# A streaming encoder layer on one core: the convolution's mean emitted later, sample heads turned later, taps held at a block's first head

## The chip, the cores and the metric

The kernel runs on one core of a Trainium2 chip. The metric is the device time of one execution in microseconds (us). A core has TensorE (matrix products, PE in the profile; PEld is its weight load), VectorE (DVE), ScalarE (ACT), GpSimd (POOL) and SyncE (SP, which only issues DMAs here). Each engine works through its own list of instructions in order, and waits on semaphores for the others.

## The reference

One layer of a hybrid encoder, on 2048 prompt frames and 64 sample frames, D_MODEL 1024. All is float32; the kernel gets that accuracy from products of split operands (a high and a low part).

```python
h = rms_norm(x, norm1_g) * (1 + sc1) + sh1          # modulated by c
glu_a, glu_b, q, k, v, g_conv, g_attn = split(h @ w_in)
u = glu_a * sigmoid(glu_b)
y = depthwise_conv(concat(hist, u), w_dw) + b_dw    # 31 taps, 512 channels
conv_out = silu(layer_norm(y)) @ w_conv_out         # mean and variance over channels
q, k = rms_norm per head(q), rms_norm per head(k)   # 8 heads of 64
o = band attention(q, k, v)                         # own chunk of 64 and the 8 before, bias, softmax
merged = sigmoid(g_conv) * conv_out + sigmoid(g_attn) * (o @ w_attn_out)
x = x + gt1 * (merged @ w_o)
x = x + gt2 * swiglu_ffn(rms_norm(x) modulated)
```

The sample frames attend to 256 cached keys and their own 64. Outputs are both x, the last 30 convolution inputs, and the keys and values kept for the next step.

## The kernel before, in words

The work has two phases. The first (to about 1220 us) goes through four token blocks: block 0 has the 64 sample rows and 512 prompt rows, blocks 1 to 3 have 512 prompt rows each. Each block runs the stages q, 0, k, 1, v, 2, 3, g: the projections to q, k and v (21 us of TensorE each, `ps<-whi,hh` and its like in the profile), four channel tiles of the gated linear unit (stages 0 to 3, `ps<-hh,whi`), and 16 gate columns (g). The second phase is the merge, the output projection and the feed-forward network, which the change does not touch.

These stages are a plain loop over TensorE's products. Everything else is woven in by a planner at build time. `Stream` keeps an estimate of each engine's load (line 163 on) and calls `tick` after each 500 ns of planned products; `tick` pumps five lanes (`Lane`, line 110): `norm_lane` (the next block's row norms), `work` (norms of q and k), `attn` (heads), `tail` (the convolution's layer norm) and `conv` (the taps). A lane holds generators. A generator yields the planned time at which it may go on, or a test; `pump` steps the first one that is ready, while the engines named in the lane's `room` are not too far ahead of TensorE. `drain` steps a lane to its end whatever the due times. The order in which instructions are emitted gives their priority to a scheduler behind it, which fixes each engine's list. Generators emit their instructions through helpers with one line (L105 in the profile), so the profile is read here by tiles.

The parts that the change touches:

- `convolve(u, y, ct, b)` (line 1224): for one channel tile one tensor_scalar and 30 fused multiply-adds on VectorE (`y<-u,wd,y`, 0.75 us for 512 columns, 0.84 for 606), one lane step each; lane `conv`, room 2000 ns on VectorE, up to four steps a tick.
- `conv_norm(y, c0, n, t0)` (line 1244), lane `tail`: waits until the `conv` lane is empty, then in all blocks but the last for MEAN_LAG. Then three additions on POOL (`s<-y`, `s<-s,y`), a product with a matrix of 1/512 that gives every partition the mean (`pm<-s,ones`), four subtractions, four squares on ScalarE, three additions on POOL (`s<-s,ln`), a second such product for the variance, square root, four reciprocals, four multiplications on POOL (`y<-y,s`), and per channel tile tanh, scale, product, split and two stores to c_d. Block 0 has two of these, first the sample's 64 columns, then the prompt's 512. Stage 0 of the next block begins with `conv.drain()` and `tail.drain()`, as `y` has one buffer.
- `attend(i)` (line 1449), lane `attn`, two heads at a time. In block 0 prompt and sample heads alternate: (0, head 0), (s, head 0), (0, head 1) and so on. A head is scored tile by tile (`sc<-kk,q` on TensorE, the maximum `pr<-sc,bias` on VectorE, the exponential on ScalarE; the tile sc has one buffer), then `scored` is set and the next head's operands are fetched. When the last tile is scaled (`pr<-pr,sm`), the head is turned: transposes (`ptp<-ident,pr`), split (`ph`, `pl`), products with V (`po<-ph,vv`), `finish_head` and the stores to o_d. Between scaling and turning it waits until TensorE's planned time has passed ScalarE's by PE_LAG.
- `heads(b)` (line 1587): 2 us after stage v it drains `work` and adds the block's heads to `attn`. At gate column 10 of block 3 (`SIDE_G`) the `conv` lane is drained.

Of the kernel before, what the change touches and what calls it, by code (L numbers as in the profile page):

```python
# [43 lines left out]
PE_LAG = 400.0  # L44
TURN_LAG = 2500.0
KN_LAG = 5000.0
X_LAG = 8000.0
MEAN_LAG = 10000.0
ON_POOL = ()
DMA_LAG = 4000.0  # L50
OUT_LAG = 4000.0
# [36 lines left out]
class Meter:  # L88


    def __init__(self, engine, name, stream):
        self.engine, self.name, self.stream = engine, name, stream
# [17 lines left out]
class Lane:  # L110
# [2 lines left out]

    def __init__(self, room, spacing=0.0, wide=1, burst=1):
        self.gens, self.room, self.spacing, self.wide, self.burst = [], room, spacing, wide, burst
        self.last = -1e9

    def add(self, gen):
        self.gens.append([gen, 0.0, {}])
# [23 lines left out]
    def pump(self, stream):  # L143
        for _ in range(self.burst):
            now = stream.load["pe"]
            if now - self.last < self.spacing or stream.full(self.room):
                return
            entry = next((e for e in self.gens[: self.wide] if self.ready(e, stream)), None)
            if entry is None:
                return  # L150
            self.last = now
            self.step(entry)
# [438 lines left out]
def streaming_layer(ctx: ExitStack, tc: tile.TileContext, I, O):  # L591
    nc = tc.nc
    stream = Stream()
    pe, dve, act, gps = (
        Meter(e, n, stream) for e, n in ((nc.tensor, "pe"), (nc.vector, "dve"), (nc.scalar, "act"), (nc.gpsimd, "pool"))
    )
# [28 lines left out]
    now = {}  # L625
# [618 lines left out]
    def conv_norm(y, c0, n, t0):  # L1244
        yv = y[:, :, c0 : c0 + n]
        yield lambda: not conv.gens
        if t0 < PBLOCKS[-1][0]:
            yield stream.load["pe"] + MEAN_LAG
        s = wk.tile([P, 512], F32, tag="ln_s", bufs=1)
# [150 lines left out]
    def spans(b):  # L1400

        if b == "s":
            return 0, SMP, 0, CACHE + SMP
        past = QB if b else 0
        return SMP + QB * b, QB, CACHE + SMP + QB * b - past, QB + past
# [11 lines left out]
    def attention(b):  # L1417

        plan(b)
        for i, head in enumerate(order):  # L1420
            if head[0] == b or b == 0:
                attn.add(attend(i))

    def plan(b):

        if (b, 0) not in order:
            order.extend((x, h) for h in range(NH) for x in ((0, "s") if b == 0 else (b,)))
# [21 lines left out]
    def attend(i):  # L1449
        x, h = order[i]  # L1450
        q0, nq, k0, nk = spans(x)
        yield lambda: now["scored"] == i - 1
        fetch(i)
        fetch_v(i)
        yield loaded[i]
        (q2, kk), (_, bias), vnow = now["qk", i], now["bias"], now["v", i]
        tiles = []
        for t in range(0, nq, P):
            n = min(P, nq - t)
            if x != 0 or t % (2 * P) == 0:  # L1460
                both = ps_a.tile([P, 2, 512], F32, tag="s", name="sc")
            ps = both if x != 0 or t % (2 * P) == 0 else both[:, 1:]
            if x not in (0, "s"):
                for j in range(2):
                    for d in range(2):
                        pe.matmul(ps[:, j, :320], q2[:, d, t : t + P], kk[:, t + 320 * j : t + 320 * j + 320], start=d == 0, stop=d == 1)
                w, src, bs = 640, ps[:, :, :320], bias[:, ::-1]
            else:
                w = nk if x == "s" else t + P
                for d in range(2):  # L1470
                    pe.matmul(ps[:n, 0, :w], q2[:, d, t : t + n], kk[:, :w], start=d == 0, stop=d == 1)
                src, bs = ps[:n, 0:1, :w], bias[:n, 64:384][:, ::-1] if x == "s" else bias[:, :w][:, ::-1]
            pr, sm, free, ready = softmax_max(src, n, w, bs)
            tiles.append((pr, sm, n, w))
            if x == 0 and t % (2 * P) == 0:
                yield stream.load["pe"], SCORE_ROOM
            elif t + P < nq:
                yield free + PE_LAG, SCORE_ROOM
            else:
                fetch(i + 1)  # L1480
                now["scored"] = i
            if t:
                softmax_scale(*tiles[-2])
        yield ready
        softmax_scale(*tiles[-1])
        yield stream.when("act") + PE_LAG
        while now["finished"] < i - 1:
            yield lambda: now["finished"] == i - 1
        fetch_v(i + 1)
        po = ps_a.tile([P, 512], F32, tag="o", name="po")  # L1490
        if x == "s":
            pt = ps_g.tile([P, 512], F32, tag="gp", name="ptp")
            ph = wk.tile([P, 512], F32R, tag="ph", name="ph", bufs=3)
            pl = wk.tile([P, 512], F32R, tag="pl", name="pl", bufs=3)
            js = ((0, P), (1, P), (2, SMP))
            for j, m in js:
                c = slice(j * SMP, j * SMP + SMP)
                pe.transpose(pt[:m, c], tiles[0][0][:SMP, j * P : j * P + m], ident[:SMP, :SMP])
            stream.after("act", "pe")
            split(ph[:, : 2 * SMP], pl[:, : 2 * SMP], pt[:, : 2 * SMP])  # L1500
            split(ph[:SMP, 2 * SMP : 3 * SMP], pl[:SMP, 2 * SMP : 3 * SMP], pt[:SMP, 2 * SMP : 3 * SMP])
            yield stream.when("dve") + PE_LAG
            for j, m in js:
                c = slice(j * SMP, j * SMP + SMP)
                for y_ in (ph, pl):
                    pe.matmul(po[:, :SMP], vnow[:m, j], y_[:m, c], start=j == 0 and y_ is ph, stop=j == 2 and y_ is pl)
        else:
            seq = (0, 1, 2, 3) if x == 0 else (3, 4, 0, 1, 2)

            def av(jj, ph, pl, _):  # L1510
                if x:
                    uses = [(jj, 0, min(jj, 3) + 1)] + ([(jj + 5, jj + 1, 4)] if jj < 3 else [])
                else:
                    uses = [(jj, jj, 4)]
                for j, a, e in uses:
                    for y_ in (ph, pl):
                        pe.matmul(
                            po[:, a * P : e * P], vnow[:, j], y_[:, a * P : e * P], start=jj == seq[0] and y_ is ph,
                            stop=jj == seq[-1] and y_ is pl and j == uses[-1][0], skip_group_check=True,
                        )  # L1520

            pend = []
            for jj in seq:
                if len(pend) > 2:
                    yield pend[0][3] + PE_LAG
                    av(*pend.pop(0))
                pt = ps_g.tile([P, 512], F32, tag="gp", name="ptp")
                t0 = 0 if x else jj
                for t in range(t0, 4):
                    j = (jj - t + (5 if t > jj else 0)) if x else jj  # L1530
                    pe.transpose(pt[:, t * P : t * P + P], tiles[t][0][:, j * P : j * P + P], ident)
                ph = wk.tile([P, 512], F32R, tag="ph", name="ph", bufs=3)
                pl = wk.tile([P, 512], F32R, tag="pl", name="pl", bufs=3)
                stream.after("act", "pe")
                w = 512 - t0 * P
                if x in ON_POOL and jj % 2:
                    p32 = temp("p32")
                    act.activation(p32[:, :w], pt[:, t0 * P :], AF.Copy)
                    act.activation(ph[:, t0 * P :], p32[:, :w], AF.Copy)
                    stream.after("pool", "act")  # L1540
                    gps.tensor_tensor(pl[:, t0 * P :], p32[:, :w], ph[:, t0 * P :].bitcast(F32), ALU.subtract)
                    pend.append((jj, ph, pl, stream.when("pool")))
                else:
                    split(ph[:, t0 * P :], pl[:, t0 * P :], pt[:, t0 * P :])
                    pend.append((jj, ph, pl, stream.when("dve")))
                yield
            for args in pend:
                yield args[3] + PE_LAG
                av(*args)
        yield stream.when("pe")  # L1550
        yield from finish_head(h, po, SMP if x == "s" else QB, q0, "s" if x == "s" else "p")
        now["finished"] = i
# [4 lines left out]
    conv, tail = Lane({"dve": CONV_ROOM}, burst=4), Lane({})  # L1557
# [17 lines left out]
    for b, stage in ORDER:  # L1575
# [7 lines left out]
        elif stage in ("q", "k", "v"):  # L1583
            qkv(b, "qkv".index(stage), norms)
            if stage == "v":

                def heads(b=b):
                    work.drain()
                    stream.flush()
                    attention(b)  # L1590
                    if b == 3:
                        attn.burst, attn.spacing = 2, 0.0

                stream.at(stream.load["pe"] + HEADS_NS, heads)
# [617 lines left out]
```

## Time and profile before

| | us |
|---|---|
| median of 3 runs (2997.07 to 3000.23) | 2997.9 |
| the profiled execution | 2997.87 |
| its span, first to last instruction | 2995.2 |
| TensorE busy / VectorE busy / ScalarE busy / POOL busy | 2910.2 / 2030.2 / 1324.2 / 942.1 |
| first phase: stage v ends in blocks 0, 1, 2, 3 at about | 165, 474, 763, 1037 |

A timeline row reads: start, length, engine, operation, output tile <- input tiles, shapes, count, and in brackets the engine's idle time before it with what ended it. A window row reads: from:to, length, then busy time (instructions) of the engines, the granted clock of TensorE as a share of full speed, the DMA engines' busy share and GB/s. A wait row reads: engine, waiting tile, what it waited for, us in total, times, longest.

### The profile page before, as it was taken

The numbers are of one execution on the slowest core, as the hardware profiler recorded it, in microseconds if no ns is written. First come the engines' busy times: TensorE is split into PE (matmuls) and PEld (weight loads), VectorE is DVE, ScalarE is ACT, GpSimd is POOL, SyncE is SP. The second block draws the span as 40 slices with busy tenths as digits, with TensorE's granted clock in tenths as the row PEclk, the third lists the DMA queues.
The fourth block names the chain that finished last, engine by engine and source line by source line (L and its number), as shares of the span: only waits on it lengthen the run. The fifth ranks groups of instructions, "written<-read, shape, count | busy, mean of one in ns | idle before, by whom it ended". The sixth has DMA issues, their size and how long they took to land.

```text
span 2995.2 us, 44652 instructions
## 1 busy us (share of the span) xinstructions
PE 2910.2 (97%) x16199; PEld 2595.7 (87%) x16199; DVE 2030.2 (68%) x3661; ACT 1324.2 (44%) x2375; POOL 942.1 (31%) x597
## 2 busy tenths in 40 slices
PE   7999989999999999989999999999999999999999
PEld 4888867887888788888999999999999898999998
DVE  5878688677866895577777755556566757366567
ACT  3344642463366257464444345434444244333332
POOL 1200120011011102355455433256656441333333
PEclk9999999999999999999999999999999999999999
DMA  8888889878987788886444786446556955355545
GB/s 299 272 290 270 290 263 304 277 251 273 306 283 248 251 268 289 267 287 235 146 153 161 253 282 230 138 141 204 189 177 213 360 197 190 117 168 176 169 155 186
DMA packets 487017, 690.95 MB, mean 231 GB/s; under 512 B 38420, under 2 KB 316808, under 8 KB 486797
## 3 DMA queue, kind: packets, MB, share of 16 engines
q1 hardware_dynamic: 469749, 662.07, 66.9%
q10 hardware_dynamic: 17048, 26.04, 2.4%
q8 instruction: 127, 2.08, 0.3%
q14 instruction: 93, 0.76, 0.1%
HBM read 503.79 MB, written 184.19 MB: 230 GB/s over the span
## 4 chain that ended last, share of the span: by engine, by line
PE 84%; DVE 8%; DMA 4%; issue 1%; POOL 1%; ACT 1%; SPq 0%; ACTq 0%; DVEq 0%; POOLq 0%
PE ps L105 55%; PE pd L105 14%; PE pw L105 6%; DVE y L105 3%; PE sc L105 2%; PE po L105 2%; PE ptp L105 2%; PE pt L105 1%; POOL r L105 1%; DVE wlo L105 1%; PE pa L105 1%; DMA wlo<-w_dfi_l 1%; DMA out<-acc 0%; DMA g_d<-gate 0%; DMA kk<-k_d 0%
## 5 line engine op out<-in xcount | busy, mean ns | idle before, releaser
L105 POOL TENSOR_TENSOR wlo<-wst,whi 128x1024 fp32r<-128x1024 f32 (+1 forms) x167 | 382.7, 2295 | 566.6 <-ACT whi L105 491.5
L105 PE MATMUL ps<-t,whi 128*128 128x384 f32 (+1 forms) x2112 | 506.0, 323 | 10.2 <-DVE t L105 6.2
L105 PE MATMUL pd<-whi,hid 128*128 128x512 f32 x1356 | 440.3, 391 | 2.7 <-DVE acc L105 2.7
L105 ACT ACTIVATE whi<-wst 128x1024 fp32r<-128x1024 f32 (+1 forms) x271 | 265.0, 982 | 376.8 <-PE ps L105 126.1
L105 PEld LDWEIGHTS ps<-t,whi 128*128 128x128 f32 x2112 | 369.7, 188 | 19.7 <-DVE t L105 7.8
L105 PE MATMUL ps<-b,whi 128*128 128x384 f32 (+1 forms) x1584 | 380.1, 326 | 4.4 <-DVE pt L105 2.4
L105 DVE SCALAR_TENSOR_TENSOR y<-u,wd,y 128x512 f32<-128x512 f32 (+1 forms) x480 | 369.2, 772 | 7.7
L105 PE MATMUL ps<-hh,whi 128*128 128x512 f32 (+2 forms) x992 | 364.8, 368 | 0.0
L105 PE MATMUL ps<-hl,whi 128*128 128x512 f32 (+2 forms) x992 | 347.7, 351 | 0.0
L105 PE MATMUL ps<-hh,wlo 128*128 128x512 f32 (+2 forms) x992 | 347.2, 350 | 0.0
L105 PE MATMUL ps<-t,wlo 128*128 128x384 f32 (+1 forms) x1056 | 340.1, 322 | 0.0
L105 DVE TENSOR_TENSOR acc<-acc,pd 128x512 f32<-128x512 f32 x440 | 289.7, 683 | 65.9 <-PE pd L105 62.3
L105 PEld LDWEIGHTS pd<-whi,hid 128*128 128x128 f32 x1356 | 254.5, 188 | 56.9 <-DVE acc L105 5.1
L105 PEld LDWEIGHTS ps<-b,whi 128*128 128x128 f32 x1584 | 277.4, 189 | 6.1 <-DVE pt L105 2.7
L105 PE MATMUL pd<-wlo,hid 128*128 128x512 f32 x700 | 273.8, 391 | 0.0
L105 PE MATMUL ps<-b,wlo 128*128 128x384 f32 (+1 forms) x792 | 256.6, 324 | 0.0
L105 ACT ACTIVATE pr<-pr,sm 128x640 f32<-128x640 f32 (+3 forms) x272 | 199.9, 746 | 121.6 <-DVE sm L105 117.7
L105 PEld LDWEIGHTS ps<-hh,wlo 128*128 128x128 f32 x992 | 188.3, 190 | 23.6 <-issue 1.2
L105 PEld LDWEIGHTS ps<-hh,whi 128*128 128x128 f32 x992 | 188.8, 190 | 20.0 <-issue 4.1
L105 PEld LDWEIGHTS ps<-hl,whi 128*128 128x128 f32 x992 | 189.2, 191 | 16.0 <-issue 2.5
L105 POOL TENSOR_TENSOR r<-t,mhalf 128x1 f32<-128x1 f32 (+3 forms) x68 | 82.0, 1208 | 378.2 <-DVE t L105 367.1
L105 PEld LDWEIGHTS ps<-t,wlo 128*128 128x128 f32 x1056 | 198.6, 188 | 0.9
(220 smaller groups left out, 5664.7 us busy)
## 6 DMA issues: line engine op xcount, KB each, us to landing
whi<-w_din_h SPq DMA_DIRECT2D x72, 512.0 KB, 5.6
wlo<-w_din_l SPq DMA_DIRECT2D x72, 512.0 KB, 7.6
wst<-sum_d SPq DMA_DIRECT2D x132, 256.0 KB, 3.0
wmod<-in_w_ada SPq DMA_DIRECT2D x48, 512.0 KB, 6.2
sum_d<-ws SPq DMA_DIRECT2D x88, 256.0 KB, 2.2
wst<-in_w_ffn_in SPq DMA_DIRECT2D x84, 256.0 KB, 3.2
wst<-in_w_in SPq DMA_DIRECT2D x40, 512.0 KB, 5.9
wst<-in_w_ffn_in SPq DMA_DIRECT2D x37, 512.0 KB, 5.5
```

The costliest lines, as they stand in the source:

```text
L105: return f(*args, **kw)
```

## The change

Three edits to the planner; no instruction is added or removed, they are emitted in another order.

1. MEAN_LAG goes from 10000 to 20000 ns: in blocks 0 to 2 the first sum of the layer norm is emitted 20 us of planned TensorE time behind the end of the taps.
2. A sample head waits SAMPLE_LAG = 3000 ns instead of PE_LAG = 400 ns between scaling and turning. Prompt heads keep 400.
3. A lane gets a flag `held`. `heads(b)` sets it on the `conv` lane, the end of any head's scoring clears it, and `pump` does nothing while it is set. `drain` does not look at it.

```diff
-MEAN_LAG = 10000.0
+MEAN_LAG = 20000.0
+SAMPLE_LAG = 3000.0
...
-        self.last = -1e9
+        self.last, self.held = -1e9, False
...
-            if now - self.last < self.spacing or stream.full(self.room):
+            if self.held or now - self.last < self.spacing or stream.full(self.room):
                 return
...
                 fetch(i + 1)
                 now["scored"] = i
+                conv.held = False
...
-        yield stream.when("act") + PE_LAG
+        yield stream.when("act") + (SAMPLE_LAG if x == "s" else PE_LAG)
...
                     attention(b)
+                    conv.held = True
```

## The prediction, made before the result was known

> **What bounds the kernel now.** I read the page first (engine shares), then the windows by stage, then the waits of TensorE, and last the timeline around each wait. The page and the windows:
>
> ```profile
> span 2995.2 us, 44652 instructions
> PE 2910.2 (97%) x16199; PEld 2595.7 (87%) x16199; DVE 2030.2 (68%) x3661; ACT 1324.2 (44%) x2375; POOL 942.1 (31%) x597
> ...
> 100.00:600.00 500.00, 468.94 (x2737) 400.16 (x2736) 381.07 (x725) 223.75 (x458) 54.55 (x59) 0.97 0.85 281
> 600.00:1000.00 400.00, 398.55 (x2231) 336.06 (x2230) 293.39 (x583) 200.99 (x371) 49.61 (x45) 1.00 0.82 263
> 1000.00:1220.00 220.00, 213.41 (x1107) 179.96 (x1106) 163.31 (x299) 116.54 (x202) 30.13 (x21) 0.99 0.85 275
> ```
>
> TensorE (first column after the length) is the bound. All three edits act on the first phase (before 1220), and there only 100 to 600 has much to give: 31.1 us without a matmul, at a granted clock of 0.97. From 600 to 1000 it idles 1.5 us. So a gain has to come from blocks 0 and 1. The waits of TensorE name three causes that the three edits address:
>
> ```profile
> PE pm L105 <- POOL s L105: 9.2, 1, 9.2
> PE sc L105 <- DVE sm L105: 9.2, 8, 3.2
> PE ptp L105 <- ACT pr L105: 7.9, 5, 4.0
> ```
>
> They sum to 26.3 us, 0.9% of the span. The profiled execution took 2997.87 us, 2.7 more than its span, and equals the median of 2997.9; I add terms to 2997.9. A change under 0.2% (6 us) can't be told from none here.
>
> **Part 1, sample heads turned 2.6 us later (3000 against 400 ns in the planner's time).** The places are the transposes of 64 rows:
>
> ```profile
> 198.74 0.58 PE L105 MATMUL ptp<-ident,pr 64*128 64x64 f32 x3 [3.97 <-ACT pr L105]
> 231.23 0.47 PE L105 MATMUL ptp<-ident,pr 64*128 64x64 f32 x3 [2.06 <-ACT pr L105]
> 447.45 0.39 PE L105 MATMUL ptp<-ident,pr 64*128 64x64 f32 x3 [0.37 <-ACT pr L105]
> 429.01 0.50 PE L105 MATMUL sc<-kk,q 128*128 128x256 f32 x2 [1.75 <-DVE sm L105]
> ...
> 200.00:204.00 4.00, 4.00 (x19) 3.94 (x17) 1.35 (x2) 0.67 (x2) 0.27 (x2) 0.50 1.03 355
> 232.00:234.00 2.00, 2.00 (x10) 2.00 (x10) 2.00 (x5) 0.24 (x2) 0.00 (x0) 0.50 0.93 255
> 204.00:208.00 4.00, 4.00 (x28) 3.75 (x29) 0.21 (x1) 0.63 (x2) 0.00 (x0) 0.99 1.01 392
> 428.00:432.00 4.00, 2.99 (x14) 2.49 (x15) 3.84 (x12) 2.08 (x7) 0.02 (x1) 1.00 0.43 140
> ```
>
> A stall costs more than its length: after the 3.97 us one the granted clock is 0.50 until about 204, some 5.3 us in which half the work is lost, 2.65 us; after the 2.06 us one some 3.2 us at 0.50 lose 1.6. After the 1.75 us stall at 429 the clock stays 1.00. So 2.6 us of matmuls put ahead of each of these transposes takes 2.60 + 2.65 from the first (1.37 us remain, under the 1.75 that left the clock alone), 2.06 + 1.6 from the second and 0.37 from the third: 9.3 us. The five other sample heads show no wait and get nothing.
>
> [...]
>
> What moves with the turn: for each of eight heads three transposes, two copies and two subtractions, six products with V, the merge, on odd heads two stores of o_d on SP, and the fetch of the next head's V (one or two loads on SP). The V load has one wait today:
>
> ```profile
> 288.35 0.47 PE L105 MATMUL po<-ph,vv 128*128 128x512 f32 x1 [0.28 <-DMA vv<-v_d]
> 452.27 0.23 DVE L105 TENSOR_TENSOR o_s<-other,po 64x64 f32<-64x64 f32 x1
> 478.13 0.74 PE L105 MATMUL sc<-kk,q 128*128 128x320 f32 x4
> ```
>
> Its next user comes after five transposes of a prompt head, so I take 0 (bounds 0 to 8 x 0.28 = 2.2 lost). The heads are turned one after another, so eight delays can push the last sample head from 452 to 473, still before block 1's first score at 478; I take 0, and price a collision below.
>
> **Part 2, the mean 20 instead of 10 us behind the last tap (blocks 0 to 2).** The one long wait on the mean is not where this delay acts:
>
> ```profile
> 302.32 0.33 PE L105 MATMUL pm<-s,ones 128*128 128x64 f32 x2
> 357.91 0.21 DVE L105 TENSOR_TENSOR part_l<-ln,part_h 128x64 fp32r<-128x64 f32 x1
> 374.11 1.02 PE L105 MATMUL pm<-s,ones 128*128 128x512 f32 x2
> 379.36 2.60 POOL L105 TENSOR_TENSOR s<-s,ln 128x512 f32<-128x512 f32 x2 [9.34 <-ACT ln L105]
> 381.91 1.64 POOL L105 TENSOR_TENSOR r<-t,mhalf 128x8 f32<-128x8 f32 x1
> 383.52 1.26 POOL L105 TENSOR_TENSOR s<-s,ln 128x512 f32<-128x512 f32 x1
> 384.84 2.08 PE L105 MATMUL pm<-s,ones 128*128 128x512 f32 x2 [9.24 <-POOL s L105]
> 385.93 1.42 PE L105 MATMUL ps<-hh,whi 128*128 128x512 f32 x1
> ...
> 385.00:388.00 3.00, 3.00 (x6) 1.57 (x7) 0.66 (x2) 1.03 (x2) 0.00 (x0) 0.50 1.10 354
> ```
>
> The second prompt product (the variance) stands directly behind the first and directly ahead of the first column product of block 1's stage 0. There the code drains the tail lane, which ignores due times. The sample's normalisation runs from its mean at 302.3 to its last split at 357.9, 55.6 us, and the prompt's waits its lag behind that. With 20 us the sample's mean comes at about 312, its end at 368, and the prompt's turn at 388, after the drain at about 375. So the drain issues the prompt's whole normalisation instead of most of it: first product, four subtractions, squares, three additions on POOL, second product. The wait of 9.24 and some 1.6 us at half clock stay. Without the 1.64 us power that got between the additions it could be 7.6; with the sample's leftovers ahead in VectorE's and ScalarE's order, and the first sums (three POOL additions of 1.1 to 1.3 us) no longer early, it could be 4 to 6 longer. I take 0, bounds 2 gained and 6 lost.
>
> In blocks 1 and 2 no product of the mean waits; all that follows moves 10 us, with eight stores of c_d on SP that are not read before the second phase. SP issues in order, so a store handed over before its split is done holds the weight loads behind it; these stores are due when the planner has the split done, before as after, and I take 0 for that. On POOL it comes up to the next block's row norms:
>
> ```profile
> 602.07 4.83 POOL L105 TENSOR_TENSOR y<-y,s 128x512 f32<-128x512 f32 x4 [12.60 <-DVE sm L105]
> 616.74 0.56 POOL L105 TENSOR_TENSOR r<-t,mhalf 128x1 f32<-128x1 f32 x1 [9.84 <-DVE t L105]
> 619.64 0.60 PE L105 MATMUL pt<-ident,x_t 128*128 128x128 f32 x4
> ```
>
> Four multiplications at 612 to 617 end about where the norm's power wants to start, and TensorE uses its result 2.3 us after that ends. Bounds: nothing, or 4.8 - 2.3 = 2.5 us in each of two blocks. I take 0.5 each, 1 us lost, as the shift of 10 leaves them just clear.
>
> **Part 3, no taps until a block's first head is scored.** In block 0 this displaces the taps beside the first scores; in block 1 there are none to displace:
>
> ```profile
> 166.80:176.50 9.70, 3.36 (x4) 1.00 0.62 209
> 188.80:196.20 7.40, 0.04 (x1) 1.00 0.66 217
> 477.00:490.00 13.00, 0.00 (x0) 1.00 0.97 394
> ...
> 172.66 0.51 PE L105 MATMUL sc<-kk,q 128*128 128x384 f32 x2
> 481.76 0.85 PE L105 MATMUL sc<-kk,q 128*128 128x320 f32 x4 [0.93 <-DVE sm L105]
> ```
>
> The first three rows are VectorE's work on the tile y alone. In block 0, 3.4 us of taps leave the stretch of the first scores, which show no wait, and go into later gaps (188.8 to 196.2 holds no tap). In block 1 the first head is scored from 478 to 484 and no tap runs before 490; the 0.93 us wait at 481.76 therefore has another cause. Blocks 2 and 3 have the order of block 1, and I take them alike. So this part gains nothing; it loses up to 3.4 us if the displaced taps stand ahead of the first sample score at 196.7. I take 0.
>
> **Sum.** -9.3 (sample turns) + 0 (drain) + 1 (POOL in blocks 1, 2) + 0 (hold) = -8.3, so 2989.6 us.
>
> **Rivals.** (a) The change doesn't do what it says: the displaced taps delay the sample's score so that the first stall keeps over 2.06 us and its half clock (gain 0.9 there instead of 5.25, in all 4), or the drain grows by 4 to 6; 2993 to 2998. For it: VectorE is the late one at 196.7; against it: it has gaps just before.
>
> (b) Slower: the later sample heads carry block 0's attention to 473, where taps fill VectorE, and block 1's first heads queue behind both. What such a head costs is seen at block 1's second head:
>
> ```profile
> 511.95 1.43 PE L105 MATMUL sc<-kk,q 128*128 128x320 f32 x4 [3.17 <-DVE sm L105]
> 514.31 1.43 PE L105 MATMUL sc<-kk,q 128*128 128x320 f32 x4 [0.93 <-DVE sm L105]
> 512.00:518.00 6.00, 4.15 (x12) 3.05 (x12) 5.81 (x12) 3.84 (x8) 0.00 (x0) 0.50 0.44 175
> 518.00:521.00 3.00, 3.00 (x14) 1.70 (x13) 2.92 (x8) 2.28 (x5) 0.00 (x0) 0.50 0.26 32
> ```
>
> Waits of 3.17 + 2 x 0.93 and half of 7.15 us of work at 0.50 give 8.6 us a head. One more such head takes the gain (2998.2), two make 3006.8. It decides from two heads on, when VectorE is over 2 us late at a score. For it: block 1 is where VectorE is late already; against it: 21 us is the most that the delays can add.
>
> (c) The other way: the shifted order frees that second head of its 8.6 us, or the drain of a few: 2981. Nothing in the change aims at it, but all order from 170 on is planned anew.
>
> **How the numbers follow.** Forecast 0.44; (a) 0.22; (b) 0.22, of it 0.06 with one such head; (c) 0.12. The forecast's own range is 2986 to 2994 (drain and POOL bounds). The whole range, 2981 to 3004, reaches into (c) and (b). Faster by over 0.2%: (c) and 0.40 of the forecast, 0.52; within: (a), the rest of the forecast and one head of (b), 0.32; slower: 0.16.
>
> **What the changed profile would show.** The waits of ptp on pr fall from 7.9 to under 3 us, and 200 to 204 is at 1.00. The 9.2 us wait of pm on s near 375 is still there, with both products in the drain. No taps at 168 to 175; the scores of blocks 1 to 3 as before. 600 to 1000 loses at most 5 us. The prediction is wrong if the pm wait goes, if the first sample turn still waits over 2 us, or if new waits of sc on sm stand at 470 to 520.

## The result, and the profile after

The changed kernel took 3006.07 us (median of 10 runs, 3002.43 to 3007.94), the kernel before 2999.10 beside it (10 runs, 2994.8 to 3002.2). The ratio is 1.0020, 95% interval 1.0012 to 1.0028: 6 us slower (7 between the two medians), where I had forecast 8.3 us faster. The price lies in the stages that the forecast had charged with 1 us, and the gain of 9.3 us in block 0 did not come.

In the page of the changed kernel the totals have hardly moved (the profiled execution took 3006.98 us):

```profile
span 3004.9 us, 44673 instructions
PE 2914.0 (97%) x16199; PEld 2599.0 (86%) x16199; DVE 2028.1 (67%) x3661; ACT 1325.6 (44%) x2375; POOL 946.2 (31%) x597
```

In its windows by stage (columns as before: TensorE, its weight load, VectorE, ScalarE, POOL, granted clock, DMA share, GB/s) the loss stands in the second:

```profile
100.00:600.00 500.00, 469.03 (x2746) 401.25 (x2745) 378.17 (x726) 222.44 (x461) 59.37 (x59) 0.97 0.84 282
600.00:1000.00 400.00, 390.50 (x2172) 328.25 (x2171) 284.16 (x566) 200.91 (x365) 47.13 (x44) 0.99 0.81 258
1000.00:1220.00 220.00, 215.55 (x1109) 180.38 (x1107) 168.34 (x308) 117.41 (x204) 29.44 (x21) 1.00 0.85 273
```

From 100 to 600 TensorE is as busy as before (468.94). From 600 to 1000 it was busy for 398.55 us and now for 390.50: 8 us more without a matmul in the stretch where I had allowed 5. The second phase begins 9.4 us later than before (its first product at 1220.83 against 1211.41), and the span is 9.7 us longer.

The waits of TensorE over the whole program, and in a second fence the timeline rows behind them:

```profile
PE sc L106 <- DVE sm L106: 13.0, 14, 2.5
PE ptp L106 <- ACT pr L106: 12.0, 11, 4.0
...
PE ps L106 <- ACT hh L106: 5.7, 3, 2.7
...
PE sc L106 <- DMA kk<-k_d: 3.0, 2, 2.8
PE pm L106 <- POOL s L106: 2.8, 1, 2.8
```

```profile
198.19 0.39 PE L106 MATMUL ptp<-ident,pr 64*128 64x64 f32 x3 [3.97 <-ACT pr L106]
...
387.01 0.80 PE L106 MATMUL sc<-kk,q 128*128 128x256 f32 x2 [2.48 <-DVE sm L106]
390.63 2.07 PE L106 MATMUL pm<-s,ones 128*128 128x512 f32 x2 [2.81 <-POOL s L106]
...
641.91 0.83 PE L106 MATMUL sc<-kk,q 128*128 128x320 f32 x4 [2.77 <-DMA kk<-k_d]
668.75 0.50 PE L106 MATMUL ps<-whi,hh 128*128 128x512 f32 x1 [2.72 <-ACT hh L106]
951.10 0.50 PE L106 MATMUL ps<-whi,hh 128*128 128x512 f32 x1 [2.72 <-ACT hh L106]
```

Four things are to be seen. The first sample turn waits 3.97 us as before. The wait of pm has shrunk from 9.24 to 2.81 us, with 2.48 of a score ahead of it. And two products of stage q, in blocks 2 and 3, wait 2.72 us each for the row norms (tile hh), where none waited before. With the 2.77 us wait of a score for its load of kk at 641.91 they make up the 8 us lost from 600 to 1000.

For each profile I summed TensorE's losses: the idle times in brackets, and half of its busy time in the stretches in which the granted clock is 0.50 (in e1 27 matmuls ran in 6.80 us at 0.50, in e5 49 in 6.60 us at 1.00, behind the same wait; both rows stand in the last section). From 150 to 620 us (from block 0's heads on, and block 1) they are 39.0 us before and 39.1 after; from 620 to the second phase 5.5 before and 15.5 after. The starts of the same stage products agree: against the kernel before they come 2.4 us earlier at 620 us and 9.4 us later at 1208. So the whole loss lies in blocks 2 and 3, and blocks 0 and 1 came out about even.

### The profile page after: what moved, and what is told of

Read it like the earlier page. It is cut to its first block, busy times and chain, and to the rows that moved or that the text cites. A ratio compares the mean times of both kernels' runs of the same rounds, so it can differ in the third digit from the quotient of the medians.

```text
span 3004.9 us, 44673 instructions
## 1 busy us (share of the span) xinstructions
PE 2914.0 (97%) x16199; PEld 2599.0 (86%) x16199; DVE 2028.1 (67%) x3661; ACT 1325.6 (44%) x2375; POOL 946.2 (31%) x597
## 3 DMA queue, kind: packets, MB, share of 16 engines
q8 instruction: 127, 2.08, 0.3%
## 4 chain that ended last, share of the span: by engine, by line
PE 79%; DVE 11%; DMA 4%; issue 2%; ACT 2%; POOL 1%; SPq 0%; ACTq 0%; DVEq 0%; POOLq 0%
PE ps L106 51%; PE pd L106 14%; PE pw L106 6%; DVE y L106 5%; PE po L106 2%; PE sc L106 2%; PE ptp L106 2%; POOL r L106 1%; DVE wlo L106 1%; PE pt L106 1%; PE pa L106 1%; DVE pr L106 0%; DMA bias<-rb_d 0%; DMA out<-acc 0%; DMA x_t<-in_x_prompt 0%
## 5 line engine op out<-in xcount | busy, mean ns | idle before, releaser
L106 ACT ACTIVATE pr<-pr,sm 128x640 f32<-128x640 f32 (+2 forms) x272 | 200.4, 747 | 119.0 <-DVE sm L106 115.8
```

What stands on the lines that cost most here:

```text
L106: return f(*args, **kw)
```

## The experiments

All ratios are to the kernel before, run beside each kernel, with their 95% intervals; 0.0010 is 3 us. "Losses" are the two sums just described.

| run | edits | ratio | losses from 150 to 620 / from 620 |
|---|---|---|---|
| before | none | 1 | 39.0 / 5.5 |
| changed kernel | all three | 1.0020 (1.0012 to 1.0028) | 39.1 / 15.5 |
| e1 | mean 20 us, all blocks | 1.0058 (1.0045 to 1.0070) | 54.9 / 15.2 |
| e2 | sample turns | 0.9997 (0.9988 to 1.0006) | 41.3 / 5.3 |
| e3 | held taps | 0.9997 (0.9987 to 1.0006) | 40.5 / 6.4 |
| e4, e8 | sample turns, held taps | 1.0021 (1.0012 to 1.0030) | 46.9 / 9.2 |
| e5 | mean 20 us in blocks 1, 2 | 1.0026 (1.0015 to 1.0036) | 41.6 / 13.6 |
| e6 | mean 20 us in block 0 | 1.0041 (1.0027 to 1.0054) | 51.3 / 9.7 |
| e7 | all, but mean 10 us in blocks 1, 2 | 0.9998 (0.9989 to 1.0006) | 41.6 / 6.1 |
| e9 | mean 15 us in blocks 1, 2 | 1.0006 (0.9998 to 1.0015) | 40.9 / 6.7 |
| e10 | mean 30 us in blocks 1, 2 | 1.0003 (0.9995 to 1.0012) | 40.3 / 8.0 |
| e11 | e5, c_d stored from ScalarE's queue | 1.0038 (1.0025 to 1.0051) | 42.5 / 22.8 |
| e12 | sample turns, mean 20 us in block 0 | 1.0007 (0.9998 to 1.0016) | 48.3 / 9.3 |
| e13 | first sample head's turn 10 us | 0.9994 (0.9985 to 1.0003) | 41.9 / 9.4 |
| e14 | mean 0 us in block 0 | 1.0018 (1.0009 to 1.0027) | 48.5 / 6.0 |
| e15 | held taps, mean 20 us in block 0 | 0.9999 (0.9990 to 1.0008) | 43.6 / 7.1 |
| e16 | first sample head's turn 15 us | 1.0041 (1.0029 to 1.0054) | 54.9 / 6.8 |
| e17 | e7, first sample head's turn 10 us | 0.9986 (0.9977 to 0.9995) | 39.5 / 11.4 |
| e18 | held taps, first sample head's turn 10 us | 1.0020 (1.0011 to 1.0029) | 53.0 / 6.4 |

The losses are those of the one profiled execution, the ratios those of medians. Set against the kernel before, the losses exceed what the ratio says by 1 to 11 us (most in e12 and e17), so they show where a kernel loses, and order the kernels only roughly.

### Which edit: one at a time

e1 to e3 are the kernel before with one edit each, e4 is the changed kernel without the first.

```diff
-MEAN_LAG = 10000.0
+MEAN_LAG = 20000.0                                                              # e1 alone
-        yield stream.when("act") + PE_LAG
+        yield stream.when("act") + (SAMPLE_LAG if x == "s" else PE_LAG)         # e2, e4
+                conv.held = False                                               # e3, e4, in attend
+                    conv.held = True                                            # e3, e4, in heads
```

The theories were M (the mean's delay makes the loss), T (the new order of heads in block 0 makes it) and S (each order has waits of its own, which do not add).

> Only the mean's delay (20 instead of 10 us); sample turns and taps as before. Theory M (the delayed mean makes the loss, by row norms and loads of blocks 2 and 3 that come late behind it): about 6 us longer than before (3005), with the two 2.7 us waits of ps on hh (669 and 951 in the changed kernel) and the 2.8 us wait of a score on the load of kk at 642 present here too, and the pm wait of block 1's stage 0 cut from 9.2 to about 3. Theory T (the later sample turns and the held taps make it, by a prompt head order in block 0 that waits more often): within 2 us of before or faster by up to 4, and none of those waits at 642, 669, 951. Theory S (no edit alone; each new order has its own waits, which do not add up): anywhere within 4 us of before.

> Only the sample heads' turns later (3000 instead of 400 ns); mean and taps as before. Theory M: 0 to 3 us faster than before, the 2.06 us wait at 231 gone and the 3.97 us wait at 199 still there, the pm wait of 9.2 us unchanged. Theory T: 3 to 7 us slower, with new waits under 1.5 us of scores and transposes at 210 to 340. Theory S: within 4 us of before.

> Only the taps held until a block's first head is scored; sample turns at 400 ns and mean at 10 us as before. Theory M: within 1 us of before. Theory T: within 2 us of before if the sample turns alone make the waits of block 0, 3 us slower if the displaced taps do. In all of them blocks 1 to 3 (from 480 us) show the same waits as before.

> The changed kernel without the mean's delay (sample turns later and taps held). Theory M: 0 to 3 us faster than before, as the sample turns alone. Theory T: as slow as the changed kernel or slower (3006 to 3010, since the drain's shorter pm wait, 3 to 6 us of gain, is lost). Theory S: within 4 us of before, and not the sum of the two edits run alone.

None of the theories holds alone. The mean's delay alone costs 17 us, three times the whole change, where M had 6, T at most 2 and S at most 4. Sample turns and held taps cost nothing each and 6 us together. So the changed kernel is not the sum of its edits. e2 shows what became of the sample turns' gain. Waits of TensorE from 190 to 530 us in e2, and two of its timeline rows:

```profile
PE sc L106 <- DVE sm L106: 13.2, 11, 3.0
PE ptp L106 <- ACT pr L106: 11.2, 11, 2.1
```

```profile
199.97 0.39 PE L106 MATMUL ptp<-ident,pr 64*128 64x64 f32 x3 [2.12 <-ACT pr L106]
...
276.80 0.56 PE L106 MATMUL sc<-kk,q 128*128 128x256 f32 x1 [3.05 <-DVE sm L106]
```

The first turn waits 2.12 instead of 3.97 us, the 2.06 us wait at 231 is gone, and no wait of pm is left at all: 13 us of waits less. Yet the time is the same: heads now wait at 212 to 348, at 378 and at 427 to 434 (eleven waits of scores instead of six, eleven of turns instead of five), and the half-clock losses from 150 to 620 rise from 10.0 to 15.0 us.

What is read from a profile of this kernel (sample turns and held taps) is read from e8, which is e4's kernel once more.

### Where: block 0, or blocks 1 and 2

The mean's delay was split by block, in the line

```diff
-            yield stream.load["pe"] + MEAN_LAG
+            yield stream.load["pe"] + (20000.0 if t0 >= PBLOCKS[0][1] else 10000.0)   # e5; e6, e7: t0 < PBLOCKS[0][1]
```

e5 and e6 start from the kernel before, e7 from the changed one.

> The kernel before with the mean 20 us behind the last tap in blocks 1 and 2 alone (block 0 keeps 10). Theory two parts (a price in blocks 1 and 2 that does not depend on how block 0 was planned, and a price in block 0 that depends on all three edits; they add): 6 to 9 us slower than before, since the shift between this edit and none grows by 6.8 us from 650 to 1220 in the changed kernel and by 8.6 with the mean's delay alone; no shift up to 620, waits of 2.7 us of ps on hh in the first products of blocks 2 and 3. Rival (the order of block 0 carries its lateness into blocks 1 to 3): within 3 us of before.

> The kernel before with the mean 20 us behind the last tap in block 0 alone (blocks 1 and 2 keep 10). Theory two parts: 9 to 12 us slower (18.2 of the mean's delay everywhere less 6 to 9), all of it before 480, with the 5.6 us wait of a score on sm near 383, and no shift added after 650. Rival: 15 to 18 us slower, with the shift still growing in blocks 2 and 3.

> The changed kernel with the mean's longer delay in block 0 alone; blocks 1 and 2 go back to 10 us. Theory two parts: 6 to 9 us less than the changed kernel, so 2997 to 3000, within 0.2% of before; the waits of ps on hh at 669 and 951 and of a score on kk at 642 are gone. Rival: within 3 us of the changed kernel (3003 to 3008).

> Sample turns later and taps held, without the mean's delay, once more for its profile. Theory two parts: the 5 us that it takes more than before are all lost before 650, in waits of scores and transposes of prompt heads, and no wait of pm stands in block 1's stage 0; from 650 to 1220 the shift against before stays within 1 us. Rival: the shift grows on in blocks 2 and 3.

The two parts separate nearly as expected. Blocks 1 and 2: 1.0026, 7.8 us. Block 0: 1.0041, 12.3 us. Their sum, 20, stands against 17.4 with both (e1). Taking blocks 1 and 2 back out of the changed kernel gives 0.9998, no difference from before, with no wait of ps on hh left in blocks 2 and 3. e8 loses most of its time before 650 as expected, with no wait of pm in stage 0; after that it shifts by 3.4 us more until 1208, not by under 1. e6 shifts by 4 us more there, where none was expected. In both a score waits 1.4 us for its load of kk near 850, and a stretch of 6.8 us at half clock follows a 2 us wait near 1025, where in the kernel before the granted clock is 1.00 from 1018 to 1035, behind its wait of 2.03 us at 1016.69; whether these belong to the kernels or to the one execution isn't shown. The 5.6 us wait foreseen for e6 is there. It is not the mean's: the maximum of the score's first tile stands on VectorE behind the norms of k, which wait for POOL's powers. VectorE's rows in e6:

```profile
374.06 0.69 DVE L105 TENSOR_TENSOR kn<-kn,r 128x512 f32<-128x512 f32 x1 [1.54 <-POOL r L105]
...
377.37 0.69 DVE L105 TENSOR_TENSOR kn<-kn,r 128x512 f32<-128x512 f32 x1 [1.81 <-POOL r L105]
377.98 0.28 DVE L105 CUSTOM_DVE_ANT_0 pr<-sc,bias 128x128 f32<-128x128 f32 x1
```

The second tile's score uses the buffer that this maximum reads. TensorE's row:

```profile
378.33 0.80 PE L105 MATMUL sc<-kk,q 128*128 128x256 f32 x2 [5.56 <-DVE sm L105]
```

So at this wait, 5.6 of the 12.3 us, the delay of the mean did its harm by where it left a prompt head, not by the mean's own steps.

### Why in blocks 2 and 3: the row norms

Two theories: rows (the last conversions of the layer norm displace the row norms of the next block) and stores (eight 256 KB stores of c_d come between the loads of heads and rows). e9 and e10 have 15000.0 and 30000.0 in place of e5's 20000.0, and e11 is e5 with

```diff
-                    nc.sync.dma_start(c_d[l, ct, :, t0 : t0 + n], a[:, :n].bitcast(F32))
+                    nc.scalar.dma_start(c_d[l, ct, :, t0 : t0 + n], a[:, :n].bitcast(F32))
```

> Mean 15 us behind the last tap in blocks 1 and 2, 10 in block 0. Theory rows (in blocks 1 and 2 the price is a step: with 20 us the last conversions of the normalisation fall on the step in which the next block's row norms are split into hh and hl, the last two rows then come 4 to 5 us later in the planner and are issued only when the product that needs them is, which waits 2.7 us): with 15 us the last conversion still ends ahead of that step, no 2.7 us wait of ps on hh at 668 and 950, within 2 us of before. Rival stores (eight 256 KB stores of c_d come between the loads of the next heads and rows on SP and on the DMA engines): the price grows with the delay, 3 to 5 us over before here.

> Mean 30 us behind the last tap in blocks 1 and 2, 10 in block 0. Theory rows: three of the conversions lie among the rows and the last row is split only at its own product: the wait of ps on hh at the start of blocks 2 and 3 is as long as with 20 us or longer, 8 to 14 us over before. Rival stores: the stores then come behind the first heads' loads of the next stage, 4 to 8 us over before, without a longer wait on hh.

> Mean 20 us behind the last tap in blocks 1 and 2, and the stores of c_d issued on ScalarE's queue instead of SP's. Theory rows: the 2.7 us waits of ps on hh stay, 6 to 9 us over before (0.3 us of ScalarE per store more). Rival stores: without the stores on SP the loads of heads and rows leave earlier, at most 2 us over before.

The row "PE ps <- ACT hh" of the waits from 620 to 1000 us, in e5, in e10 and in e11 (one fence each); e9 and the kernel before have no such row:

```profile
PE ps L105 <- ACT hh L105: 5.5, 2, 2.7
```

```profile
PE ps L105 <- ACT hh L105: 1.5, 2, 0.8
```

```profile
PE ps L105 <- ACT hh L105: 9.0, 2, 4.5
```

With 10, 15, 20 and 30 us of delay the waits are 0, 0, 5.5 and 1.5 us, and the times 0, +1.8, +7.8 and +0.9 us over before. With the stores moved to ScalarE's queue the waits are 9.0 us and the time is +11.4. The time follows this wait in all five, within 3 us. The changed kernel and e1, which have 20 us there too, have 5.4 and 5.5 us of it; of the other kernels, with 10 us there, none has any. Stores on SP's queue are therefore not the cause, since moving them made it worse; that the same stores, as transfers, slow something was not tested, and with them ScalarE, which rounds the rows, got more to issue. Rows was wrong too, in what it said of 30 us and in the size of e11. The price does not grow with the delay, it is paid at one setting. What differs is where the third row's transposes stand, in e5 (first fence) and in the kernel before (second):

```profile
645.43 0.60 PE L105 MATMUL pt<-ident,x_t 128*128 128x128 f32 x4
664.32 1.03 PE L105 MATMUL pt<-ident,x_t 128*128 128x128 f32 x8
668.08 0.50 PE L105 MATMUL ps<-whi,hh 128*128 128x512 f32 x1 [2.73 <-ACT hh L105]
```

```profile
641.71 0.60 PE L105 MATMUL pt<-ident,x_t 128*128 128x128 f32 x4
652.67 0.66 PE L105 MATMUL pt<-ident,x_t 128*128 128x128 f32 x4
657.87 0.60 PE L105 MATMUL pt<-ident,x_t 128*128 128x128 f32 x4
```

Before, the third row's eight transposes come in two fours at 652.67 and 657.87, with other products between them and the product that needs them. In e5 all eight stand together at 664.32, directly ahead of the product that needs their result: `qkv` calls `norm_lane.drain` ahead of each row's products, so a row that is undone is finished on the spot. The affine on VectorE (behind a head's maximum) and the rounding on ScalarE then lie bare, 2.73 us. With 30 us the first four come at 653.53 again. That the conversions keep the planner from starting the row is argued from the order, not shown by a run.

### Whether a wait in block 0 is worth its length

e12 and e15 complete the eight combinations of the three edits in block 0. They are e2 and e3 with e6's line:

```diff
-            yield stream.load["pe"] + MEAN_LAG
+            yield stream.load["pe"] + (20000.0 if t0 < PBLOCKS[0][1] else 10000.0)
```

> Sample turns later, and the mean 20 us behind the last tap in block 0 alone; taps not held. Theory two parts, with fixed prices of the edits in block 0 (sample 0, mean 10.9): 11 us over before. Rival (in block 0 an edit has no price of its own; the drain at block 1's stage 0 and the heads meet anew in each order): the mean's products stand in the drain here with a score between them as in the changed kernel, so nearer to that kernel's block 0, within 4 us of before.

> Taps held, and the mean 20 us behind the last tap in block 0 alone; sample turns as before. Theory price (each edit has its own in block 0: hold 0, mean 10.9): 11 us over before. Rival (the price belongs to the order as a whole): within 4 us of before, as with the sample turns and the mean.

In us over before (ratio times 3000): sample -0.9, hold -0.9, mean +12.3, sample and hold +6.3, sample and mean +2.1, hold and mean -0.3, all three -0.6. A price of its own for each edit is refuted: the mean's delay costs 12 us alone and takes 7 away from the other two.

e13 and e16 remove the first sample turn's wait alone. In the kernel before, in the changed one, in e2 and in e3 the turn stands directly behind its score on TensorE's list, with no matmul between. In the kernel before the score stands about where its operands come in: its load on SP's queue, its own row, and the line on the loads of kk from 155 to 260 us (one fence each):

```profile
191.61 0.60 SPq L1366 DMA_DIRECT2D kk<-k_d  x1
```

```profile
194.28 0.48 PE L105 MATMUL sc<-kk,q 128*64 128x320 f32 x2
```

```profile
DMA to landing us min/median/max: 2.5/2.5/2.6
```

191.61 + 2.5 is 194.1: the score starts within 0.2 us of the landing. The load alone does not fix the place, though: in e2 the load is issued at 191.70 and the score starts at 197.41, and the turn still stands directly behind it. What holds the two together isn't shown; a lag of 3 us did not part them. With 10 us there are 36 matmuls between (16 when the later sample heads have 3 us, in e17, and when taps are held, in e18).

```diff
-        yield stream.when("act") + PE_LAG
+        yield stream.when("act") + (10000.0 if x == "s" and h == 0 else PE_LAG)     # e16: 15000.0
```

> The kernel before, with a lag of 10 us instead of 0.4 on the first sample head's turn alone. In the three kernels with 3 us the turn still stood directly behind its score, since the score itself was placed late, behind its loads; with 10 us there are 36 matmuls (4.8 us) between them. Theory price (a wait and its half clock are worth what they take): the 3.97 us wait at 199 and its half clock go, 4 to 7 us faster than before. Rival (in block 0 what one wait gives back is taken by others, as the order behind it is planned anew): the wait goes, and the time stays within 2 us of before, with new waits of scores and transposes between 210 and 480.

> As the lag of 10 us on the first sample head's turn, with 15 us: 98 matmuls between the score and its turn. Theory price: as much faster as with 10 us, within 2 us, since the wait is gone in both. Rival: not the same as with 10 us; the two differ by over 2 us, as the order of block 0 differs.

In e13 the first wait is gone and so is the 9.2 us one of pm, 13 us of waits and their half clock. The time fell by 1.8 us, which the interval can't tell from nothing. In their place, the waits of TensorE from 190 to 530 and, in the second fence, one row of the timeline of e13:

```profile
PE ptp L105 <- ACT pr L105: 10.9, 6, 4.3
PE sc L105 <- DVE sm L105: 10.6, 9, 3.2
```

```profile
414.35 0.58 PE L105 MATMUL ptp<-ident,pr 64*128 64x64 f32 x3 [4.27 <-ACT pr L105]
```

A later sample head waits 4.27 us where none did. With 15 us (e16) the kernel is 12.3 us slower, though both old waits are gone there too.

e14 does the same to the wait of pm, with a delay of 0 in block 0 (`0.0 if t0 < PBLOCKS[0][1] else MEAN_LAG`).

> The kernel before with no delay of the mean in block 0 (0 instead of 10 us; blocks 1 and 2 keep 10). The prompt's normalisation is then issued ahead of block 1's stage 0 and the 9.2 us wait of pm is gone. Theory price: the wait and its half clock are worth 11 us, so 5 to 11 us faster than before. Rival: within 3 us of before, with other waits in the first rows and products of block 1.

No pm waits in the drain any more (2.7 us are left, at 299), and the kernel is 5.4 us slower, which neither expectation had: a score waits 4.50 us for its load at 295, and turns and scores wait 23 us in all. TensorE's waits in e14 from 190 to 530, and that row:

```profile
PE sc L105 <- DVE sm L105: 11.7, 10, 3.2
PE ptp L105 <- ACT pr L105: 11.1, 7, 4.0
PE sc L105 <- DMA kk<-k_d: 5.7, 2, 4.5
PE pm L105 <- POOL s L105: 2.7, 1, 2.7
```

```profile
295.57 0.66 PE L105 MATMUL sc<-kk,q 128*128 128x128 f32 x2 [4.50 <-DMA kk<-k_d]
```

### A version with both causes taken away

e17 is e7 and e18 is e3, each with the 10 us for the first sample head.

> The changed kernel with the mean's longer delay in block 0 alone and a lag of 10 us on the first sample head's turn (3 on the others): the price of blocks 1 and 2 and the first wait are both taken away. Theory price: 4 to 6 us faster than before. Rival (no wait of block 0 is worth its length once the order changes): between 4 faster and 12 slower; which of them can't be told ahead, only that TensorE's waits and half-clock losses from 150 to 620 account for it within 2 us.

> The kernel before with taps held and a lag of 10 us on the first sample head's turn alone; mean as before. Theory price: 4 to 7 us faster than before, as the first wait goes. Rival: between 4 faster and 12 slower, accounted for within 2 us by the waits and half-clock losses from 150 to 620.

e17 is the fastest kernel here, 2996.87 us, 0.9986 (0.9977 to 0.9995), 4.2 us under before; its interval overlaps that of e7 (0.9989 to 1.0006). e18 is 6 us slower than before. In both the first sample turn's wait went to the next prompt head, whose load of kk is now late (e17, TensorE's waits from 190 to 530, and the row):

```profile
PE sc L106 <- DMA kk<-k_d: 6.4, 1, 6.4
PE pm L106 <- POOL s L106: 5.6, 1, 5.6
```

```profile
212.69 0.66 PE L106 MATMUL sc<-kk,q 128*128 128x128 f32 x2 [6.43 <-DMA kk<-k_d]
```

So e17 does not win by the wait that it was to remove. That the time came out at the 4 to 6 us of the theory is luck. I had expected the losses from 150 to 620 to account for the difference within 2 us. By the starts of the same stage products e17 gains 2.2 us there, where its losses are 0.5 higher than before, and e18 loses 10, where they are 14 higher: they miss by 2.7 and 4 us.

## Why the prediction was wrong, point by point

- **Part 1, 9.3 us gained: failed, at two steps.** "2.6 us of matmuls put ahead of each of these transposes" does not follow from a later due time. At the first head it did not happen at all: the turn still stood right behind its score (3.97 us again). At 231.23 and 447.45 the waits did go, as worked out (the half clock of the second belonged to one execution, see the end). The second step is the one that matters: that a wait removed is time gained. The waits of ptp on pr, forecast to fall from 7.9 to under 3 us, rose to 12.0: the first turn's 3.97, and the rest on prompt heads. With its half clock I had priced the first wait at 6.6 us, and that of pm comes to 10.8 by the same reckoning. e13, without either, gained nothing, and e14, without the second, lost 5.4. The idle time of TensorE from 150 to 620 is 26 to 35 us in all 19 profiles, 29.0 before; what varies more is the half-clock loss, 10 to 24.
- **Part 2, block 0's drain, 0 (bounds -2 and +6): failed.** The wait of pm did not stay at 9.24: it became 2.48 and 2.81. Alone (e6) the same delay costs 12.3, over the upper bound. Both ends came from counting the normalisation's own steps in the drain; the longest wait of e6 is a prompt head's.
- **Part 2, blocks 1 and 2, 1 us (bounds 0 and 5): the place was right, the mechanism and the size were not.** I looked at POOL's power; it ran when asked (at 656.20 in e5, 8 us ahead of the row's transposes at 664.32). The row's transposes came too late on TensorE's list, and what follows them lay bare, 2.7 us in each of the two blocks. In the changed kernel the granted clock is 0.50 from 669.99 to 673.40, behind the first of the two waits, and 1.00 from 951 to 955, behind the second. 7.8 us by e5, and this term alone takes the changed kernel from 0.9998 to 1.0020.
- **Part 3, 0: right for the edit alone, and luck beside the others.** e3 is at 0.9997, and from 649 to 1208 us it stands within 0.4 us of the kernel before, so the edit does nothing that shows in blocks 2 and 3. But beside the sample turns the same edit costs 7 us (e4 against e2), and beside the mean's delay in block 0 it takes 12 to 13 away (e15 against e6), so a term of its own, which the sum needs, does not exist. The sign named for it was wrong: four taps still run from 166.8 to 176.5 (VectorE's work on the tile y, below), as many as before. Four are missing further on, 20 in place of 24 by 215.

```profile
166.80:176.50 9.70, 3.23 (x4) 1.00 0.64 218
```

- **Rivals.** (b) gave 3006.8, and 3006.07 came, but not by its mechanism: block 1's second head waits 1.61, 1.62 and 1.57 us, 4.8 in all, where it waited 5.0. (a) was half right, in that the first stall stayed. 600 to 1000 lost 8 us where I had allowed 5, and no rival named that.

## What to carry to other kernels

When a build-time planner fixes the order, a due time is not a place: before you price a shift, see whether the instruction really comes to stand elsewhere on the engine's list (here 3 us moved the first turn past no matmul, 10 us past 36). A stall may be counted as gain only if nothing else is late behind it; here every order had 26 to 35 us of them in blocks 0 and 1, and the times of orders that differ by one constant lay up to 14 us apart. A loss that stays where it is, whatever else is changed (the row norms that stage q drained), is the one worth finding: look for work that is forced out right ahead of the product that needs it.

## What the runs showed of the hardware

The same wait does not cost the same clock. The first sample turn waits 3.97 us in e5 and 3.98 in e1, with the same matmuls behind it. In e5's windows (first fence) the granted clock is 0.50 for one stretch of 3.4 us, in e1's (second) for three:

```profile
198.40:201.80 3.40, 3.40 (x15) 3.23 (x16) 2.52 (x5) 1.32 (x3) 0.45 (x2) 0.50 1.07 269
201.80:208.40 6.60, 6.60 (x49) 6.31 (x48) 1.68 (x7) 1.13 (x4) 0.00 (x0) 1.00 0.96 375
```

```profile
198.20:201.60 3.40, 2.82 (x12) 2.65 (x13) 2.71 (x4) 1.85 (x4) 0.45 (x2) 0.50 1.06 231
201.60:208.40 6.80, 6.80 (x27) 6.33 (x27) 0.62 (x3) 0.63 (x2) 0.00 (x0) 0.50 0.96 376
```

At 0.50 e1 gets through 27 matmuls in 6.80 us, at 1.00 e5 through 49 in 6.60. With half of the busy time at 0.50 taken as lost, that is 1.7 us in the one and 4.8 in the other. In e1 the wait reaches into the first of the three, in which TensorE is busy for 2.82 of 3.40 us; in e5 it ends as the stretch begins. The second sample turn's wait of 2.06 us, which I priced with 1.6 us of half clock, costs no clock in e1, e5, e6 and e14, where it is 2.06 to 2.08 us long. In e5, its timeline row, and the window behind it with that behind a wait of 1.78 us at 429.85:

```profile
230.06 0.39 PE L105 MATMUL ptp<-ident,pr 64*128 64x64 f32 x3 [2.08 <-ACT pr L105]
```

```profile
230.10:234.00 3.90, 3.90 (x29) 3.73 (x30) 3.23 (x8) 2.02 (x5) 0.00 (x0) 1.00 1.08 295
...
430.50:433.90 3.40, 3.40 (x10) 2.83 (x9) 2.43 (x9) 1.71 (x5) 0.00 (x0) 0.50 0.06 24
```

The longer wait leaves the clock at 1.00 and the shorter one halves it. So there is no threshold between 1.75 and 2.06 us, as I had taken it from one profile. The half-clock stretches of the first phase last 3.41, 6.83 or 10.24 us in the kernel before and 3.41 or 6.83 in the changed one (17.0 from 208.5 to 225.5 in e17), and in each profile their starts lie on one grid of 3.413 us: before at 74.39, 115.35, 197.27, 231.40, 378.17 and 511.29, which is 12, 24, 10, 43 and 39 times 3.413 us apart, and in the changed kernel at 72.66, 198.95, 216.02, 338.90, 386.68, 512.98, 642.68 and 669.99, which is 37, 5, 36, 14, 37, 38 and 8 times. In these profiles, how much of such an interval TensorE was busy told more than the length of a wait. In the kernel before the 2.06 us wait at 231.23 falls into one interval (first fence), and the next one is at half clock. In e5 the same wait is split between two (second fence), and none follows:

```profile
228.00:231.40 3.40, 1.34 (x11) 1.03 (x10) 2.16 (x6) 1.63 (x4) 0.00 (x0) 1.00 0.66 227
231.40:234.80 3.40, 3.40 (x17) 3.23 (x16) 2.68 (x5) 0.62 (x3) 0.00 (x0) 0.50 0.92 236
```

```profile
225.70:229.10 3.40, 2.28 (x18) 1.96 (x16) 1.08 (x3) 0.94 (x3) 0.00 (x0) 1.00 0.53 120
229.10:232.50 3.40, 2.44 (x19) 2.35 (x19) 3.37 (x8) 1.52 (x6) 0.00 (x0) 1.00 1.01 298
```

Counted over all 19 profiles from 150 to 1210 us, of the intervals at full clock, those with TensorE busy for under 0.44 were followed by half clock in 89 of 89 cases, those with 0.44 to 0.65 in 27 of 113, and those with more in 1 of 5460. In the profiles of the kernel before and of the changed one alone it was 9 of 9, 2 of 10 and 0 of 581.
